# Splitting fp32 weights into hi and lo: by VectorE, or by two transfers and ScalarE

## The chip, the cores and the metric

The kernel runs on 1 core of one Trainium2 chip. The time is device microseconds of one execution; the time before is 799.55 us, the median of 3 runs (799.49 to 800.0). Engines are named as in the profile: PE (TensorE), with PEld for its weight loads, DVE (VectorE), ACT (ScalarE), POOL (GpSimd) and SP (SyncE, which only issues transfers).

## What is computed

One post-norm encoder layer on 512 tokens of width 1024, all in float32. Two token mixers work on the same input: windowed grouped-query attention (A) and a mixture of three dilated attentions (B). Sigmoid gates merge them; then a SwiGLU of width 2816.

```python
proj = h @ w_in[l]
qa, ka, va, qb, kb, vb = jnp.split(proj, SPLITS, axis=-1)
...
o_a = windowed_gqa_sink(qa, ka, va, a_sink[l])
o_b = dilated_mixture(qb, kb, vb)
gates = jax.nn.sigmoid(h @ w_gate[l] + b_gate[l])
g_a, g_b = jnp.split(gates, N_BRANCH, axis=-1)
mixed = g_a * (o_a @ w_br_a[l]) + g_b * (o_b @ w_br_b[l])
h = layer_norm(DN_ALPHA * h + mixed @ w_out[l], ln1_g[l], ln1_b[l])
f = (jax.nn.silu(h @ w_ff_gate[l]) * (h @ w_ff_up[l])) @ w_ff_down[l]
h = layer_norm(DN_ALPHA * h + f, ln2_g[l], ln2_b[l])
```

## The kernel before

**Products.** Each operand of a large product is split into two parts that the PE takes in one pass each: hi, the operand rounded to the type float32r, and lo, what is left of it. A product is three matmuls: hi by hi, hi by lo, lo by hi (`feat_k`, lines 432 to 434; in `tok_major`, 959 to 961). So each weight must be split before it is used.

**Weights.** They lie in HBM as units of 128x1024, and a unit is fetched as two half units of 128x512 (256 KB). `half_unit` makes one: SP loads it to a slot of class `ws`, `split` copies it with rounding to h (ACT or DVE, lines 312 and 314), and DVE subtracts h from it into l (line 336). h and l lie in slots of class `whl`. 152 half units go this way: all projections, the gates, the branch and output projections, the first three and the last two of 22 feed-forward blocks, and the last four rows of down units. The first four half units of the program are cut into pieces instead (`half_unit_by`, 355 to 361). Most feed-forward blocks (`quad`) and most down units (`Chunk`) use a Strassen-like scheme with sums of weights: for those, `load_sum` loads one weight and has POOL issue a second transfer that adds another to it (line 326). These remain.

**Order.** No engine's order is written by hand. Operations are recorded with the engines that may do them, costs, priorities and what they read and write; `Program.run` then plays them through by those costs and gives each engine its instructions in the order in which they would start. At run time each engine keeps that order and waits for semaphores. `pr.limits` says how many slots each class may hold at once (85 in all; `N_WS` for `ws`, `N_WHL` for `whl`, the rest for general use), and two operations of no cost change those limits between stages. A half unit's priority is that of a matmul 130 us earlier (`LOOK`).

**Stages**, by the profile: start and first projections, then attention A and B between further projections and gates up to 361 us, branch and output projections with the first layer norm up to about 451, feed-forward blocks, and the last down units with the second layer norm from about 745 on. At the end of the output projection each block of 128 tokens is normalised and turned (`turn_h1`: four PE transposes of line 1026, then ACT and DVE copies), while the PE goes on with the next block.

Of the kernel before, what the change touches and what calls it, by code (L numbers as in the profile page):

```python
# [9 lines left out]
F32 = mybir.dt.float32  # L10
F32R = mybir.dt.float32r
BF16 = mybir.dt.bfloat16
AF = mybir.ActivationFunctionType
ALU = mybir.AluOpType

P = 128
S = 512
# [4 lines left out]
NR = 4  # L22
# [34 lines left out]

FIRST = ((-1000, -998), (-997.5, -996), (-993.5,), (-992.5,),
         (-999, -997, -995, -994, -993, -992, -991, -990))
N_WS, N_WHL, N_ATT = 6, 12, 16  # L60


QUADS = range(3, 20)
# [30 lines left out]
class Program:  # L94
# [15 lines left out]
    def op(self, alts, fn, reads=(), writes=(), prio=0.0, after=(), abs_prio=None, moves=0.0):  # L110
        o = Op()
        o.alts, o.fn = alts, fn
        o.prio = (self.T + prio if abs_prio is None else abs_prio, len(self.ops))
        o.ready, o.done, o.eng = 0.0, None, None
        deps = set(a for a in after if a is not None)
        for t in reads:
            deps.update(self.writer.get(t, ()))
        for t in writes:
            deps.update(self.writer.get(t, ()))
            deps.update(self.readers.get(t, ()))  # L120
        deps.discard(o)
# [12 lines left out]
        o.succ = []  # L134
        o.left = len(deps)
        for d in deps:
            d.succ.append(o)
        self.ops.append(o)
        return o
# [118 lines left out]
def act(n, psum=False, extra=0):  # L258
    return (0.052 if psum else 0.094) + 0.000833 * n + 0.093 * extra
# [11 lines left out]
def hybrid_layer(ctx: ExitStack, tc: tile.TileContext, wpack, xT, xtok, sink, bgate,  # L271
                 ln1g, ln1b, ln2g, ln2b, ropec, ropes, maska, maskb, identd, out):
    nc = tc.nc
# [9 lines left out]
    op = pr.op  # L283
# [7 lines left out]
    def slot(dt=F32, cls=None):  # L291
        cls = cls or "gen"
        return Buf("slot", cls, lambda: slab.tile([P, S], dt, tag="slab", bufs=N_SLOT, name=name("sl")))
# [16 lines left out]
    def copy(eng, dst, src):  # L310
        if eng == ACT:
            nc.scalar.activation(dst, src, AF.Copy)  # L312
        else:
            nc.vector.tensor_copy(dst, src)

    def f32(ap):
        return ap.bitcast(F32)

    def load(b, src, cost=0.73, prio=0.0, abs_prio=None, dst=None, after=()):
        return op([(SP, cost)], lambda e: nc.sync.dma_start(dst() if dst else b.t, src), writes=[b],  # L320
                  prio=prio, abs_prio=abs_prio, after=after)
# [7 lines left out]
    def cp_alts(n, ps=False):  # L329
        return [(ACT, act(n, ps)), (DVE, dve(n, not ps))]  # L330

    def split(src, h, l, prio=0.0, abs_prio=None, hold=()):

        op(cp_alts(S), lambda e: copy(e, h.t, src.t), reads=[src], writes=[h, *hold], prio=prio,
           abs_prio=abs_prio)
        op([(DVE, dve(S))], lambda e: nc.vector.tensor_tensor(l.t, src.t, f32(h.t), op=ALU.subtract),  # L336
           reads=[src, h], writes=[l], prio=prio, abs_prio=abs_prio)
# [1 line left out]
    LOOK, LOOK_W, LOOK_U, LOOK_T = 130.0, 30.0, 15.0, 15.0  # L339

    def half_unit(u, j):
        st, h, l = slot(F32, "ws"), slot(F32R, "whl"), slot(F32R, "whl")
        load(st, wpack[u, :, j * S:(j + 1) * S], prio=-LOOK)
        split(st, h, l, prio=-LOOK, hold=[(l, "room")])
        return h, l

    pieces = {}

    def half_unit_by(u, j, cuts, prios):

        st, h, l = slot(F32, "ws"), slot(F32R, "whl"), slot(F32R, "whl")
        pieces[h] = pieces[l] = cuts
        for (c0, c1), ap in zip(cuts, prios):
            w = c1 - c0
            op([(SP, 0.73 * w / S)], lambda e, c0=c0, c1=c1: nc.sync.dma_start(
                st.t[:, c0:c1], wpack[u, :, j * S + c0:j * S + c1]), writes=[(st, c0)], abs_prio=ap)
            op(cp_alts(w), lambda e, c0=c0, c1=c1: copy(e, h.t[:, c0:c1], st.t[:, c0:c1]),
               reads=[(st, c0)], writes=[(h, c0), (l, "room", c0)], abs_prio=ap)
            op([(DVE, dve(w))], lambda e, c0=c0, c1=c1: nc.vector.tensor_tensor(
                l.t[:, c0:c1], st.t[:, c0:c1], f32(h.t[:, c0:c1]), op=ALU.subtract),  # L360
               reads=[(st, c0), (h, c0)], writes=[(l, c0)], abs_prio=ap)
        return h, l
# [471 lines left out]
    def dense_k(u, nt):  # L834
        ps = bank("dense")
        feat_x(ps, unit(u))
        return k_post(ps, nt)
# [12 lines left out]
    def step(w):  # L850
        if w == "VA":
            env["va"] = turned_values(U_VA, 4)
        elif w[0] == "q":
            i = int(w[1])
            kv = (i // 2) % 2
            qa.extend(dense_q(U_QA + i, 4, (kv, kv)))
        elif w == "k1":
            ka.extend(dense_k(U_KA + 1, 4))
        elif w[0] == "A":
            g = int(w[1])  # L860
            for b in range(NR):
                unit_a(g, b, qa[4 * g:4 * g + 4], ka[g], env["va"])
        elif w[0] in "gG":
            for _ in range(int(w[1:] or 1)):
                gate(env["gate"], w[0] == "G")
                env["gate"] += 1
        elif w[0] in "QK":
            pair, g = int(w[1]), int(w[2])
            u = U_QKB + 6 * pair + 2 * g + (w[0] == "K")
            if w[0] == "Q":  # L870
                env["qs"][pair, g] = dense_q(u, 4 if g == 0 else 0, (0, 1))
            else:
                env["ks"][pair, g] = dense_k(u, 8 if g == 0 else 0)
        elif w == "V0":
            env["v0"] = turned_values(U_V0, 8, 1)
        elif w[0] == "V":
            env["v" + w[1]] = token_values(U_VB + 2 * int(w[1]) - 2)
        elif w[0] == "B":
            hs = int(w[1])
            unit_b(hs, [env["qs"][hs // 2, g][hs % 2] for g in range(3)],  # L880
                   [env["ks"][hs // 2, g][hs % 2] for g in range(3)], env["v0"], env["v1"], env["v2"])
# [4 lines left out]
    op([(POOL, 0.0)], lambda e: pr.limits.update(gen=N_SLOT - N_WS - N_WHL, whl=max(N_WHL, 4 * N_LAST1 + 4)), after=lasts)  # L886


    def split_of(src, toks, prio=0.0):
        h, l = slot(F32R), slot(F32R)  # L890
        op(cp_alts(S), lambda e: copy(e, h.t, src.t), reads=toks, writes=[h, (l, "room")], prio=prio)
        op([(DVE, dve(S))], lambda e: nc.vector.tensor_tensor(l.t, src.t, f32(h.t), op=ALU.subtract),
           reads=[*toks, h], writes=[l], prio=prio)
        return h, l
# [8 lines left out]
    for f in range(16):  # L903
        op([(ACT, act(S))], lambda e, f=f: nc.scalar.activation(gz[f].t, gz[f].t, AF.Sigmoid),
           reads=[gz[f]], writes=[gz[f]], after=exps)
    sa = [split_of(t, [(t, b) for b in range(NR)], -20) for t in oaT]
    MA = moving(sa)
    sm = []
    mark = None
# [543 lines left out]
```

## Time and profile before

| | |
|---|---|
| median of 3 runs | 799.55 us |
| profiled execution, its time | 799.82 us |
| its span, first to last instruction | 797.7 us |
| PE, DVE, ACT, POOL busy | 98%, 83%, 56%, 11% |
| DMA queue of SP: data, share of 16 engines | 91.53 MB, 35.0% |
| DMA queue of POOL: data, share of 16 engines | 13.63 MB, 10.4% |

Busy times by stretch, and the share of the 16 DMA engines:

| us | DVE | ACT | POOL | DMA |
|---|---|---|---|---|
| 0 to 437 | 351.92 | 264.86 | 46.20 | 0.35 |
| 437 to 490 | 48.96 | 29.90 | 6.13 | 0.57 |
| 490 to 740 | 221.23 | 145.93 | 37.21 | 0.71 |
| 740 to 798 | 41.14 | 9.22 | 0.00 | 0.10 |

How to read it: matmuls are pipelined, and one counts as busy while its columns run through, so 98% doesn't say that the PE issues all the time; what its weight loads waited for says more. The granted clock was full almost throughout (0.996). The share of the DMA engines is a mean over the stretch.

### The profile page before, as it was taken

The page shows a single profiled execution, that of the slowest core. Times are in us where ns is not written, and L with a number is a line of the kernel's source. Part 1 is how long each engine was busy: PE and PEld are TensorE (multiplying, and loading weights), DVE is VectorE, ACT ScalarE, POOL GpSimd, SP SyncE. Part 2 cuts the span into 40 slices and gives each one's busy share as a digit, 9 for nine tenths or more (in the row PEclk, how much of TensorE's full clock was granted, in tenths as well). Part 3 has the DMA queues.
Part 4 walks back from the last instruction along what each step waited for, and adds up shares of the span by engine and source line. Part 5 has one row for each costly group of instructions (what it writes and reads, how often), then busy time and mean ns, then how long its engine had stood idle before and what let it go on. Part 6 is the DMA issues. An engine that isn't in the chain of part 4 may idle for free.

```text
span 797.7 us, 13253 instructions
## 1 busy us (share of the span) xinstructions
PE 784.7 (98%) x4598; PEld 690.3 (87%) x4598; DVE 663.3 (83%) x1385; ACT 449.9 (56%) x980; POOL 89.5 (11%) x256
## 2 busy tenths in 40 slices
PE   8999999999999999999999999999999999999995
PEld 5888888888899888888888899999999999998884
DVE  6998989999955699858495988699898989898858
ACT  5577665758755663767151555555556546566310
POOL 0000000000033100420000011111121211100000
PEclk9999999999999999999999999999999999999998
DMA  8423132242032132328442458666986857846002
GB/s 291 171 93 102 55 109 67 80 146 66 27 106 68 51 107 68 122 91 306 155 144 68 135 143 199 158 171 151 227 224 173 204 147 209 242 153 178 1 19 87
DMA packets 58674, 106.00 MB, mean 133 GB/s; under 512 B 6768, under 2 KB 7792, under 8 KB 58608
## 3 DMA queue, kind: packets, MB, share of 16 engines
q1 hardware_dynamic: 51120, 91.53, 35.0%
q0 software_dynamic: 7488, 13.63, 10.4%
q8 instruction: 36, 0.59, 0.3%
q14 instruction: 30, 0.25, 0.1%
HBM read 100.68 MB, written 4.46 MB: 132 GB/s over the span
## 4 chain that ended last, share of the span: by engine, by line
PE 89%; DVE 6%; ACT 2%; DMA 1%; issue 1%; SPq 0%; DVEq 0%; ACTq 0%
PE ps L433 13%; PE ps L432 13%; PE ps L434 13%; PE ps L1156 7%; PE ps L1155 7%; PE ps L1154 7%; PE ps L1293 4%; PE ps L1294 4%; PE ps L1295 4%; PE ps L608 3%; PE ps L961 2%; PE ps L959 2%; PE ps L960 2%; PE ps L517 2%; PE ps L516 2%; ACT sl L312 1%
## 5 line engine op out<-in xcount | busy, mean ns | idle before, releaser
L312 ACT ACTIVATE sl<-sl 128x512 fp32r<-128x512 f32 (+3 forms) x404 | 226.4, 593 | 102.2 <-DVE sl L458 42.9
L432 PE MATMUL ps<-x,sl 128*128 128x512 f32 (+1 forms) x464 | 174.4, 376 | 0.6 <-ACT x L312 0.6
L433 PE MATMUL ps<-x,sl 128*128 128x512 f32 (+1 forms) x464 | 171.5, 370 | 0.2 <-DVE x L408 0.2
L434 PE MATMUL ps<-x,sl 128*128 128x512 f32 (+1 forms) x464 | 171.1, 369 | 0.0
L312 ACT ACTIVATE sl<-ps 128x256 f32<-128x256 f32 (+5 forms) x169 | 76.3, 468 | 116.4 <-PE ps L1156 72.6
L1065 DVE TENSOR_TENSOR sl<-sl,sl 128x512 fp32r<-128x512 f32 (+3 forms) x246 | 137.9, 599 | 4.6 <-ACT sl L312 3.3
L336 DVE TENSOR_TENSOR sl<-sl,sl 128x512 fp32r<-128x512 f32 x152 | 101.4, 686 | 6.0 <-ACT sl L312 3.7
L434 PEld LDWEIGHTS ps<-x,sl 128*128 128x128 f32 x464 | 87.6, 189 | 15.0
L432 PEld LDWEIGHTS ps<-x,sl 128*128 128x128 f32 x464 | 87.8, 189 | 13.5 <-ACT x L312 1.7
L433 PEld LDWEIGHTS ps<-x,sl 128*128 128x128 f32 x464 | 87.8, 189 | 13.1 <-DVE x L408 1.4
L1156 PE MATMUL ps<-sl,sl 128*128 128x256 f32 x272 | 77.0, 283 | 0.0
L1155 PE MATMUL ps<-sl,sl 128*128 128x256 f32 x272 | 77.0, 283 | 0.0
L1154 PE MATMUL ps<-sl,sl 128*128 128x256 f32 x272 | 77.0, 283 | 0.0
L326 POOL DMA_DIRECT2D sl<-wpack x34 | 29.5, 867 | 281.9 <-PE ps L960 75.2
L1156 PE MATMUL ps<-x,sl 128*128 128x256 f32 x204 | 57.7, 283 | 0.0
L1155 PE MATMUL ps<-x,sl 128*128 128x256 f32 x204 | 57.7, 283 | 0.0
L1154 PE MATMUL ps<-x,sl 128*128 128x256 f32 x204 | 57.7, 283 | 0.0
L1154 PEld LDWEIGHTS ps<-sl,sl 128*128 128x128 f32 x272 | 52.2, 192 | 0.2
L1155 PEld LDWEIGHTS ps<-sl,sl 128*128 128x128 f32 x272 | 52.2, 192 | 0.2
L1156 PEld LDWEIGHTS ps<-sl,sl 128*128 128x128 f32 x272 | 52.2, 192 | 0.0
L1293 PE MATMUL ps<-sl,sl 128*128 128x512 f32 x126 | 49.3, 391 | 0.0
L1294 PE MATMUL ps<-sl,sl 128*128 128x512 f32 x126 | 49.3, 391 | 0.0
(135 smaller groups left out, 1623.4 us busy)
## 6 DMA issues: line engine op xcount, KB each, us to landing
sl<-wpack SPq DMA_DIRECT2D x239, 256.0 KB, 3.5
wf<-wpack SPq DMA_DIRECT2D x54, 256.0 KB, 4.3
sl<-wpack POOLq DMA_DIRECT2D x34, 256.0 KB, 5.2
wf<-wpack POOLq DMA_DIRECT2D x18, 256.0 KB, 7.0
gz<-sl SPq DMA_DIRECT2D x9, 256.0 KB, 2.1
sl<-gz SPq DMA_DIRECT2D x9, 256.0 KB, 4.7
sl<-xT SPq DMA_DIRECT2D x8, 256.0 KB, 5.5
sl<-xtok SPq DMA_DIRECT2D x8, 256.0 KB, 5.3
```

The costliest lines, as they stand in the source:

```text
L312: nc.scalar.activation(dst, src, AF.Copy)
L336: op([(DVE, dve(S))], lambda e: nc.vector.tensor_tensor(l.t, src.t, f32(h.t), op=ALU.subtract), reads=[src, h], writes=[l], prio=prio, abs ...
L432: mm(o, a, x0, start=(k == 0), stop=False)
L433: mm(o, a, x1, start=False, stop=False)
L434: mm(o, b, x0, start=False, stop=(k == nk - 1))
L1065: op([(DVE, dve(w))], lambda e: nc.vector.tensor_tensor(dst(), x(), y(), op=o), reads=reads, writes=writes, prio=prio)
L1154: mm(o, wh, bh[k](), start=(first and k == 0), stop=False, skip_group_check=True)
L1155: mm(o, wh, bl[k](), start=False, stop=False, skip_group_check=True)
L1156: mm(o, wl, bh[k](), start=False, stop=(k == 3), skip_group_check=True)
L1293: mm(ps.t, x0, w[0].t, start=(first and m == 0), stop=False, skip_group_check=True)
L1294: mm(ps.t, x0, w[1].t, start=False, stop=False, skip_group_check=True)
L1295: mm(ps.t, x1, w[0].t, start=False, stop=(m == N_PAIR - 1), skip_group_check=True)
```

## The change

A half unit no longer uses a `ws` slot, SP, or DVE. POOL issues a transfer that casts the weight from float32 to float32r on its way into h. ACT writes -h into l (`activation` with scale -1). POOL then issues a second transfer of the same weight that adds it to l, so l is w - h. Each of the three waits for the one before. `N_WS` goes from 6 to 0 and `N_WHL` from 12 to 16; pieces of the first half units take general slots. The splits of A's outputs now also wait for the K projection of the second pair of B heads.

```diff
-N_WS, N_WHL, N_ATT = 6, 12, 16
+N_WS, N_WHL, N_ATT = 0, 16, 16
...
     def half_unit(u, j):
-        st, h, l = slot(F32, "ws"), slot(F32R, "whl"), slot(F32R, "whl")
-        load(st, wpack[u, :, j * S:(j + 1) * S], prio=-LOOK)
-        split(st, h, l, prio=-LOOK, hold=[(l, "room")])
+
+        h, l = slot(F32R, "whl"), slot(F32R, "whl")
+        src = wpack[u, :, j * S:(j + 1) * S]
+        op([(POOL, 1.0)], lambda e: nc.gpsimd.dma_start(h.t, src), writes=[h, (l, "room")], prio=-LOOK, moves=0.73)
+        op([(ACT, act(S))], lambda e: nc.scalar.activation(l.t, f32(h.t), AF.Copy, scale=-1.0), reads=[h],
+           writes=[l], prio=-LOOK)
+        op([(POOL, 1.0)], lambda e: nc.gpsimd.dma_start(l.t, src, accum_op=ALU.add), reads=[l], writes=[l],
+           prio=-LOOK, moves=0.73)
         return h, l
...
     def half_unit_by(u, j, cuts, prios):
-        st, h, l = slot(F32, "ws"), slot(F32R, "whl"), slot(F32R, "whl")
+        st, h, l = slot(F32, "xs"), slot(F32R, "whl"), slot(F32R, "whl")
...
                 env["ks"][pair, g] = dense_k(u, 8 if g == 0 else 0)
+                env["k", pair, g] = pr.ops[-1]
...
-    sa = [split_of(t, [(t, b) for b in range(NR)], -20) for t in oaT]
+    sa = [split_of(t, [(t, b) for b in range(NR)], -20, [env["k", 1,0]]) for t in oaT]
```

In the changed kernel the cast is line 345, the negation 346, the adding transfer 348; lines further down stand 5 or 6 later than before. How instructions stand on two engines at two places:

ACT at the start, before. `sl` slots fed from `wpack` are weights, `x` is the input; each row waits for a load of SP (DMAHW).

```order
L312 ACTIVATE sl20_121<-sl1_72 128x128 [waits DMAHW0_49]
L312 ACTIVATE x422_127<-sl2_74 128x512 [waits DMAHW1_49]
L312 ACTIVATE sl20_121<-sl1_72 128x384 [waits DMAHW2_49]
L312 ACTIVATE sl24_132<-sl3_77 128x128 [waits DMAHW3_49]
L312 ACTIVATE x422_127<-sl4_79 128x512 [waits DMAHW4_49]
L312 ACTIVATE sl24_132<-sl3_77 128x384 [waits DMAHW5_49]
```

The same in the changed kernel; DMASW is a transfer issued by POOL.

```order
L312 ACTIVATE sl26_129<-sl3_75 128x128 [waits DMAHW0_49]
L312 ACTIVATE x428_135<-sl4_77 128x512 [waits DMAHW1_49]
L346 ACTIVATE sl2_73<-sl1_72 128x512 [waits DMASW0_49]
L312 ACTIVATE sl32_144<-sl5_80 128x128 [waits DMAHW3_49]
L312 ACTIVATE x428_135<-sl6_82 128x512 [waits DMAHW4_49]
L312 ACTIVATE sl32_144<-sl5_80 128x384 [waits DMAHW5_49]
```

A negation of a weight that is used later stands third, ahead of the first piece of the q weights and the second tile of x.

ACT before, at the end of the output projection: `ps1114` is a turned half of the second token block, `ps1140` of the third; the rows from `sl1115` on copy feed-forward weights to h.

```order
L312 ACTIVATE sl1111_4966<-ps1114_5010 128x2x128
L312 ACTIVATE sl1115_5039<-sl1086_4808 128x512
L312 ACTIVATE sl1117_5046<-sl1087_4817 128x512
L991 ACTIVATE st1113_5008<-st1113_5008,eps_68 128x1
L312 ACTIVATE sl1119_5055<-sl1092_4836 128x512
L312 ACTIVATE sl1121_5062<-sl1093_4841 128x512
L312 ACTIVATE sl1124_5071<-sl1098_4872 128x512
L312 ACTIVATE sl1127_5080<-sl1099_4877 128x512
L312 ACTIVATE sl1132_5101<-sl1123_5065 128x512
L312 ACTIVATE sl1136_5112<-sl1126_5074 128x512
L312 ACTIVATE sl1138_5122<-sl1129_5083 128x512
L312 ACTIVATE sl1142_5136<-sl1130_5089 128x512
```

The same place in the changed kernel: `ps982` is a half of the second block, `ps991` and `ps995` are those of the third.

```order
L312 ACTIVATE sl979_4828<-ps982_4872 128x2x128
L997 ACTIVATE st981_4870<-st981_4870,eps_68 128x1
L312 ACTIVATE x4970_4801<-ps991_4932 128x4x128
L346 ACTIVATE sl984_4902<-sl983_4901 128x512
L312 ACTIVATE sl996_4957<-ps991_4932 128x2x128
L346 ACTIVATE sl986_4911<-sl985_4910 128x512
L312 ACTIVATE sl997_4965<-ps991_4932 128x2x128
L312 ACTIVATE sl998_4967<-ps995_4947 128x2x128
L346 ACTIVATE sl988_4922<-sl987_4921 128x512
L312 ACTIVATE sl1000_4979<-ps995_4947 128x2x128
L346 ACTIVATE sl990_4930<-sl989_4929 128x512
L346 ACTIVATE sl994_4945<-sl993_4944 128x512
```

Before, ten weights were copied ahead of the third block's turn; now five negations stand among its copies. Only two half units of this stage are negated earlier.

More of the change, by code (lines that the diff above doesn't have):

```diff
@@ L886, in hybrid_layer, with split_of @@
     op([(POOL, 0.0)], lambda e: pr.limits.update(gen=N_SLOT - N_WS - N_WHL, whl=max(N_WHL, 4 * N_LAST1 + 4)), after=lasts)
-    def split_of(src, toks, prio=0.0):
+    def split_of(src, toks, prio=0.0, after=()):
         h, l = slot(F32R), slot(F32R)
-        op(cp_alts(S), lambda e: copy(e, h.t, src.t), reads=toks, writes=[h, (l, "room")], prio=prio)
+        op(cp_alts(S), lambda e: copy(e, h.t, src.t), reads=toks, writes=[h, (l, "room")], prio=prio, after=after)
         op([(DVE, dve(S))], lambda e: nc.vector.tensor_tensor(l.t, src.t, f32(h.t), op=ALU.subtract),
```

## The prediction

> **What bounds the kernel now.** The page first: how long the span is, who fills it, and on what the chain that ended last lies.
>
> ```profile
> span 797.7 us, 13253 instructions
> ...
> PE 784.7 (98%) x4598; PEld 690.3 (87%) x4598; DVE 663.3 (83%) x1385; ACT 449.9 (56%) x980; POOL 89.5 (11%) x256
> ...
> PE 89%; DVE 6%; ACT 2%; DMA 1%; issue 1%; SPq 0%; DVEq 0%; ACTq 0%
> ```
>
> TensorE holds the chain, but VectorE (DVE) is 83% busy and has 6% of it, so relief of VectorE could be worth something. How much, the waits of TensorE's weight loads (PEld) say: a matmul that has to wait shows there first. Columns: who waited, for whom, us in total, times, longest.
>
> ```profile
> PEld ps L608 <- ACT sl L596: 2.3, 6, 1.0
> PEld ps L432 <- ACT x L312: 1.7, 2, 1.0
> ...
> PEld ps L433 <- DVE x L408: 1.4, 3, 0.5
> ...
> PEld ps L654 <- DVE sl L613: 1.1, 3, 0.4
> PEld ps L1026 <- DVE sl L1008: 0.8, 2, 0.4
> PEld ps L777 <- DVE sl L613: 0.7, 1, 0.7
> PEld ps L802 <- DVE sl L613: 0.5, 1, 0.5
> ```
>
> L432 and L433 wait at the start, for x; L1026 waits in the first layer norm, which the change leaves alone. What is left hangs on the attention's elementwise chain: 2.3 + 1.1 + 0.7 + 0.5 = 4.6 us. That is the whole room below: the chain's 6% on VectorE runs beside matmuls that go on issuing. Stretches of 20 us show the same (TensorE, its weight loads, DVE, ACT, POOL busy, then clock, DMA share and GB/s):
>
> ```profile
> 180.00:200.00 20.00, 19.90 (x93) 16.03 (x92) 19.59 (x41) 16.83 (x32) 1.59 (x4) 1.00 0.20 66
> 200.00:220.00 20.00, 19.26 (x109) 16.44 (x108) 18.52 (x45) 14.55 (x35) 0.61 (x4) 1.00 0.10 27
> ...
> 400.00:420.00 20.00, 20.00 (x90) 16.54 (x89) 16.87 (x28) 9.49 (x16) 0.00 (x0) 1.00 0.48 159
> 420.00:440.00 20.00, 20.00 (x93) 16.27 (x91) 12.08 (x21) 2.97 (x8) 1.87 (x2) 1.00 0.24 52
> ```
>
> VectorE is full at 180 to 220, and TensorE still issues; at 400 to 440 nothing holds it. So a late weight costs its full lateness, and nothing later gives it back.
>
> **What is removed.** For each of 152 half units (128x512 weights) a load on SP's queue, one copy and one VectorE subtraction:
>
> ```profile
> L336 DVE TENSOR_TENSOR sl<-sl,sl 128x512 fp32r<-128x512 f32 x152 | 101.4, 686 | 6.0 <-ACT sl L312 3.7
> ...
> sl<-wpack SPq DMA_DIRECT2D x239, 256.0 KB, 3.5
> ```
>
> 101.4 us leave VectorE. The copies become negations on ScalarE (ACT), one for one, so its load stays. Of the 4.6 us above, 2.3 have ScalarE as releaser, and it stays as loaded; the other 2.3 wait for VectorE's L613. I take -3.0 for the relief, with 0 and -4.6 as ends: what is late next there is ScalarE's softmax.
>
> **What is added.** 304 transfers on POOL's queue, two in series for each half unit with a ScalarE instruction between. The nearest rows are the present accumulating transfers (L326): POOL's time for an issue, then issue to landing (min/median/max), and what the two queues' packets took.
>
> ```profile
> L326 POOL DMA_DIRECT2D sl<-wpack x34: 862/862/1007, 421.1 to 677.1; - x34
> L326 POOL DMA_DIRECT2D wf<-wpack x18: 862/865/1294, 476.0 to 720.3; - x18
> ...
> DMA to landing us min/median/max: 3.7/5.5/9.7
> ...
> q1 hardware_dynamic: 51120, 91.53, 35.0%
> q0 software_dynamic: 7488, 13.63, 10.4%
> ...
> L312 ACT ACTIVATE sl<-sl 128x512 fp32r<-128x512 f32 x282 | 166.7, 623 | 50.8 <-DVE sl L929 16.7 <-DVE sl L1191 8.1 <-DVE sl L1065 7.3
> ```
>
> A weight is then ready 5.5 + 0.62 + 5.5 = 11.6 us after its first issue, against 3.5 + 0.62 + 0.69 = 4.8 now. POOL: 304 x 0.86 = 261 us over the span, so it isn't full. The transfers: 35.0% of 797.7 us for 91.53 MB is 3.05 us/MB, 0.80 us of all 16 engines for a plain 256 KB; 10.4% for 13.63 MB is 1.60 us for an accumulating one. No row shows a casting transfer: 0.80 is its lower end, 1.60 its upper. It moves the bytes of a plain one and reads no destination, so I take 0.80. A half unit then needs 2.40 us of the engines, and TensorE uses one up in 12 matmuls of 512 columns. Their pace is in the chain's pieces (start, us, what):
>
> ```profile
> 444.16 0.23 PE ps L959
> ...
> 219.51 0.12 PE ps L581
> ...
> 441.65 0.44 PE ps L1026 x4
> ```
>
> 12 x 0.23 = 2.76 us, more where attention lies between. It fits, at 87% of the engines in the dense stretches. There the lead decides. By the changed order an accumulating transfer is mostly released 20 to 30 us of TensorE's work ahead of its use, against some 8 us (negation, issue, landing): these cost nothing while the lead holds. Four places have less.
>
> *Start.* ScalarE's second copy is now followed by a negation that waits for the first casting transfer, ahead of the q weights' first piece and the second x tile. What gates TensorE there now:
>
> ```profile
> 0.75 0.38 SPq L355 DMA_DIRECT2D sl<-wpack  x1
> ...
> 5.47 0.31 ACT L312 ACTIVATE sl<-sl 128x128 fp32r<-128x128 f32 x1 [0.36 <-DMA sl<-wpack]
> ...
> 7.12 0.63 ACT L312 ACTIVATE x<-sl 128x512 fp32r<-128x512 f32 x1 [1.34 <-DMA sl<-xT]
> ...
> 4.00:6.00 2.00, 2.00 (x5) 0.87 (x4) 1.34 (x3) 1.38 (x3) 0.00 (x0) 1.00 0.84 243
> 6.00:8.00 2.00, 1.43 (x6) 0.84 (x4) 0.33 (x2) 0.88 (x2) 0.00 (x0) 1.00 0.92 281
> ```
>
> Issued at about 1 us, as SP's first is at 0.75, and landed 5.5 later, with 0.62 and 0.31 of ScalarE: x can be copied at 7.4 instead of 7.1, if it is there. With 9.7 it is 11.6, 4.5 late. The engines are 84 to 92% busy then, and five casting transfers (1.3 MB) join the x loads. I take +2.0, between 0 and +4.5.
>
> *Branch projections.* The last attention head is done some 15 us of TensorE's work ahead of the first use of the add released by it; POOL's queue then has nine casting transfers ahead of the next adds, beside the 21 loads of gates, x and layer norm vectors. 5 x 1.60 + 9 x 0.80 is 15 us of engine time, and half of the 21 loads 8: 23 us against 26 to the use of the tenth. Each add still lands late after that: +1.0, 0 to +4.
>
> *Into the feed-forward part.* This is the largest. Before, ScalarE had copied these weights ahead of the third token block's turn; now five negations stand behind that block's copies. From the block's transposes to the first matmul that reads the first of these lo parts, TensorE's order has 12 matmuls of 512, one more group of four transposes and 26 matmuls of 256: 12 x 0.23 + 0.44 + 26 x 0.12 = 6.3 us. Against that the turn's copy 0.60 (quoted next), a negation 0.62, and the landing.
>
> ```profile
> L312 ACT ACTIVATE x<-ps 128x512 fp32r<-128x512 f32 x8 | 4.8, 598 | 13.2 <-PE ps L1026 13.2
> ```
>
> With 5.5 that is 6.7, 0.4 us late; with 9.7 it is 10.9, 4.6 late. SP's queue holds 19 loads for the feed-forward part right behind the layer norm vectors, with nothing but free buffers to hold them, so I go near the contended end: +4.0. Five more follow at 12 x 0.12 = 1.44 us each in the first pass, about as fast as an add moves (1.60): the upper end is +8.
> [...]
>
> *Last down weights.* Four adds are released 7.9 to 10 us ahead; a subtraction, a split copy, a negation and a landing make 0.69 + 0.62 + 0.62 + 5.5 = 7.4. The engines are idle there: +0.3, 0 to +2.
>
> SP loses 152 loads, which only brings its later loads forward. The 18 + 34 accumulating loads of the feed-forward part keep more than 30 us of lead. POOL's small attention copies now stand between transfers and wait for softmax; their waits are inside the leads above. That some gates' splits now also wait for a K projection costs nothing: that is long done.
>
> **Sum**, against the profiled execution's own 799.82 (797.7 of span and 2.1 around it): 799.82 - 3.0 + 2.0 + 1.0 + 4.0 + 0.3 = 804.1. It was 0.27 above the median of 799.55, so 803.9, said as 804.
>
> **Rivals.**
> *The leads hold (faster, 0.24).* Landings stay near 5.5 everywhere, the start loses 0.3, the feed-forward entry 0.4, and the relief brings up to 4.6: 799.6 - 4.6 + 0.7 = 795.7. For it: the median landing; VectorE full at 180 to 220. It decides at a landing of about 6 us: below, the relief is larger than the lateness.
> *They cancel (0.14).* Terms of 2 to 4 us both ways: 798.0 to 801.1, within 0.2% (1.6 us), about what a measurement of this kernel can tell from no change.
> *A casting transfer moves like an accumulating one (slower, 0.07).* Then a half unit needs 3.20 us against 2.76. From the branch projections to the feed-forward part 28 casting and 27 adding transfers and 21 loads make 55 x 1.60 + 21 x 0.80 = 105 us in about 87 of TensorE's work: 18 us more, 822. Against it: it reads no destination.
> *VectorE's copies hold up POOL's issues (slower, 0.03).* An issue took at most 1.29 us against 0.86, so the trace bears out 0.4. Were it several times that at each of the three tight places, with five adds in a row, it would be 10 us: 814.
> [...]
> That the change doesn't do what it says is no rival: the order shows 152 subtractions fewer on VectorE.
>
> **How the numbers follow.** The forecast itself has 0.52, and its band is 801.2 to 814. Faster is the first rival, 0.24. Same is 0.14. Slower is 0.52 + 0.07 + 0.03 = 0.62. The range runs from 796.5 to 814: it takes in the slower ends of the start, branch and feed-forward terms singly, not all together (818), and leaves out 822 and the best of the first rival.
>
> **What would show it.** VectorE's busy time near 562 us with L336's group gone; POOL's issues 356; TensorE waiting for DMA landings at 5 to 12 us, around 365 to 380 and at 445 to 455; its waits at 188 to 212 and 360 shrunk. It is wrong if no weight load waits for a landing of wpack, if the waits in the attention grow (ScalarE queued behind late casting transfers), or if landings on POOL's queue have a median above 8 us through the whole first half.

## The result, and the profile after

The changed kernel takes 847.54 us (median of 4 runs, 842.3 to 849.08) against 799.75 beside it: a ratio of 1.0588, 95% interval 1.0572 to 1.0604, so 48 us slower where 4 were forecast. The profiled execution took 849.08 us. Its page: span, busy time by engine, the two data queues (packets, MB, share of 16 engines), and the shares of the chain that ended last.

```profile
span 847.2 us, 13441 instructions
...
PE 808.2 (95%) x4598; PEld 706.2 (83%) x4598; DVE 580.0 (68%) x1237; ACT 451.0 (53%) x976; POOL 297.8 (35%) x560
...
q0 software_dynamic: 51264, 93.35, 55.7%
q1 hardware_dynamic: 29232, 51.67, 18.5%
...
PE 54%; issue 15%; DMA 10%; POOL 9%; DVE 7%; ACT 4%; SPq 1%; POOLq 0%; DVEq 0%; ACTq 0%
```

The change did to VectorE what it says: 663.3 us became 580.0 (83 less, not the 101 of the subtractions: its copies, L314, took some 7 us more, and the rest was not followed up). But TensorE's share of the chain fell from 89% to 54%, and landings and GpSimd, which had 1% and nothing, have 19%. The waits of the changed kernel (who, for whom, us in total, times, longest):

```profile
POOL sl L348 <- ACT sl L346: 220.8, 76, 19.4
ACT sl L346 <- DMA sl<-wpack: 101.3, 45, 6.9
...
DVE st L747 <- POOL st L740: 28.5, 4, 16.4
...
PEld ps L439 <- DMA sl<-wpack: 7.6, 3, 3.4
...
PEld ps L613 <- ACT sl L601: 6.5, 9, 2.7
...
PEld ps L966 <- DMA sl<-wpack: 6.0, 4, 3.6
...
PEld ps L521 <- issue: 4.7, 1, 4.7
```

Read from the top it looks like a chain of queues: the add (L348) holds GpSimd for the negation, the negation (L346) holds ScalarE for the cast's landing, VectorE's merge of attention B (L747) waits for GpSimd's small copies (L740), and TensorE waits for all three: for landed weights (L439, L966), for softmax (L613) and for A's first scores (L521). Not every wait in it costs time: the longest of VectorE's four for L740, 16.4 us, ended at 288 us, in a stretch that lost nothing. In stretches of the changed kernel (TensorE, its loads, DVE, ACT, POOL, clock, DMA share, GB/s):

```profile
0.00:20.00 20.00, 14.92 (x39) 8.02 (x40) 7.99 (x17) 8.19 (x14) 5.01 (x12) 1.00 0.99 302
40.00:60.00 20.00, 15.66 (x67) 13.04 (x66) 10.17 (x29) 10.38 (x27) 10.56 (x21) 0.83 0.81 171
320.00:340.00 20.00, 17.70 (x92) 15.03 (x90) 13.45 (x36) 14.06 (x31) 8.46 (x16) 0.85 0.86 156
380.00:400.00 20.00, 16.58 (x74) 14.07 (x73) 12.12 (x27) 15.45 (x30) 4.55 (x8) 0.74 0.82 227
440.00:460.00 20.00, 16.95 (x75) 13.70 (x73) 1.41 (x3) 5.24 (x9) 9.82 (x13) 1.00 0.88 183
480.00:520.00 40.00, 32.96 (x219) 30.85 (x218) 24.12 (x40) 17.52 (x35) 18.46 (x23) 0.91 0.99 255
```

The first and the last of these stretches in the kernel before:

```profile
0.00:20.00 20.00, 18.00 (x64) 11.94 (x65) 12.32 (x24) 11.70 (x19) 1.22 (x12) 1.00 0.87 291
...
480.00:520.00 40.00, 40.00 (x336) 40.00 (x335) 30.43 (x57) 22.92 (x49) 6.04 (x7) 1.00 0.77 181
```

TensorE issued 39 matmuls instead of 64 in the first 20 us, and 219 instead of 336 at 480 to 520. The clock, 1.00 before, was granted at 0.74 to 0.91 in four of these stretches.

A finer measure is used below for every kernel: the distance between the starts of neighbouring matmuls, less a base (0.2265 us at 512 columns, 0.116 at 256, 0.0625 at 128), summed where it is over 0.02 us. The medians of the kernel before are 0.227, 0.120 and 0.109, so the base at 128 is an allowance of the author's that stands well below the measured pace. What lies at 1.6 to 2.2 times the base, in matmuls of 256 and 512 columns, counts as slow pace (in brackets), the rest as waits. Matmuls of 128 columns at half pace (0.21 us apart at 334 to 335 us in the changed kernel, 0.11 at 346 to 347) are among the waits, so the brackets are a lower bound. Much of 60 to 310 is the normal pace of short matmuls and transposes: of the 16.1 us of the kernel before, some 9.5 are distances at 128 columns that lie less than 0.1 us above the base. Stretches are fixed in time, so in a shorter kernel an event can slide over an edge.

| kernel | median us | 0–60 | 60–310 | 310–400 | 400–530 | 530 on | of it slow pace |
|---|---|---|---|---|---|---|---|
| before | 799.6 | 6.2 | 16.1 | 6.1 | 2.3 | 0 | (3.3) |
| changed | 847.5 | 18.8 | 14.4 | 25.6 | 18.3 | 2.3 | (13.9) |
| e1 real landing times | 833.5 | 15.0 | 15.1 | 15.8 | 12.0 | 1.1 | (10.1) |
| e2 merge copies on VectorE | 843.6 | 18.7 | 21.5 | 11.4 | 22.8 | 0.8 | (15.2) |
| e3 first units old way | 845.1 | 14.4 | 16.0 | 25.9 | 16.6 | 0.9 | (12.4) |
| e5 = e1 + e2 | 833.9 | 15.7 | 19.3 | 9.5 | 14.6 | 1.2 | (9.3) |
| e6 cast alone | 810.4 | 15.6 | 15.9 | 7.8 | 2.8 | 0 | (5.8) |
| e7 add alone | 810.0 | 10.7 | 16.0 | 5.5 | 5.4 | 1.3 | (4.0) |
| e8 = e3 + x first | 833.2 | 5.7 | 15.4 | 28.0 | 17.6 | 0.8 | (11.1) |
| e9 late units old way | 835.1 | 19.0 | 20.2 | 23.4 | 2.4 | 0 | (10.2) |
| e10 all four cures | 805.4 | 6.0 | 19.4 | 9.6 | 2.4 | 0 | (3.2) |
| e11 middle only | 799.2 | 5.5 | 15.8 | 5.8 | 2.3 | 0 | (3.4) |
| e12 cast alone, x first | 799.5 | 5.8 | 16.1 | 6.4 | 2.7 | 0 | (3.5) |
| e13 landing 10 us | 843.3 | 19.9 | 18.2 | 14.3 | 15.7 | 1.8 | (12.1) |
| e14 = e10, copies on GpSimd | 809.6 | 5.4 | 15.5 | 17.5 | 2.4 | 0 | (4.5) |

The changed kernel's row is 48.7 us above that of before, its span 49.5. So the loss lies in three places: the first 60 us (+12.6), 310 to 400 (+19.5), and 400 on (+18.3). In the middle it gained 1.7. Of the whole, at least 10.6 us are slow pace. The granted clock gives another figure: its mean was 0.971 over 847.2 us and 0.996 over 797.7 us before, so 24.6 and 3.2 us of full clock were withheld. By that up to some 21 us of the loss can be slow pace; this is an estimate, and the half pace of the first microseconds (matmuls of 512 columns 0.43 us apart at 11.4 to 12.7 us, where the granted clock reads 1.00) is not in it.

### The profile page after: what moved, and what is told of

Same layout as the page of the kernel before. It is cut to its first block, busy times and chain, and to the rows that moved or that the text cites. A ratio compares the mean times of both kernels' runs of the same rounds, so it can differ in the third digit from the quotient of the medians.

```text
span 847.2 us, 13441 instructions
## 1 busy us (share of the span) xinstructions
PE 808.2 (95%) x4598; PEld 706.2 (83%) x4598; DVE 580.0 (68%) x1237; ACT 451.0 (53%) x976; POOL 297.8 (35%) x560
## 4 chain that ended last, share of the span: by engine, by line
PE 54%; issue 15%; DMA 10%; POOL 9%; DVE 7%; ACT 4%; SPq 1%; POOLq 0%; DVEq 0%; ACTq 0%
DMA sl<-wpack 9%; PE ps L1162 7%; PE ps L1161 7%; PE ps L1160 7%; PE ps L437 6%; PE ps L439 6%; PE ps L438 6%; POOL sl L348 4%; POOL sl L345 3%; PE ps L1300 3%; PE ps L1299 3%; PE ps L1301 3%; ACT sl L312 2%; PE ps L613 2%; DMA sl<-xT 1%
## 5 line engine op out<-in xcount | busy, mean ns | idle before, releaser
L348 POOL DMA_DIRECT2D sl<-wpack x152 | 136.5, 973 | 292.9 <-ACT sl L346 220.8
L312 ACT ACTIVATE sl<-sl 128x512 fp32r<-128x512 f32 (+3 forms) x261 | 142.7, 576 | 78.0 <-DVE sl L463 28.0
L439 PE MATMUL ps<-x,sl 128*128 128x512 f32 (+1 forms) x464 | 174.8, 377 | 7.0 <-DMA sl<-wpack 7.0
L437 PE MATMUL ps<-x,sl 128*128 128x512 f32 (+1 forms) x464 | 178.0, 384 | 2.2 <-DVE sl L314 1.9
L438 PE MATMUL ps<-x,sl 128*128 128x512 f32 (+1 forms) x464 | 175.2, 378 | 1.7 <-DVE x L413 1.7
L346 ACT ACTIVATE sl<-sl 128x512 fp32r<-128x512 f32 x152 | 93.8, 625 | 102.3 <-DMA sl<-wpack 101.3
L345 POOL DMA_DIRECT2D sl<-wpack x152 | 116.1, 940 | 13.6 <-DMA sl<-wpack 5.6
L312 ACT ACTIVATE sl<-ps 128x256 f32<-128x256 f32 (+6 forms) x157 | 69.9, 457 | 94.9 <-PE ps L1162 69.7
L439 PEld LDWEIGHTS ps<-x,sl 128*128 128x128 f32 x464 | 90.4, 195 | 23.4 <-DMA sl<-wpack 7.6
L437 PEld LDWEIGHTS ps<-x,sl 128*128 128x128 f32 x464 | 90.2, 194 | 16.9 <-issue 2.3
L438 PEld LDWEIGHTS ps<-x,sl 128*128 128x128 f32 x464 | 90.3, 195 | 15.2 <-DVE x L413 3.1
L326 POOL DMA_DIRECT2D sl<-wpack x34 | 29.7, 963 | 164.2 <-DMA sl<-wpack 62.0
```

Source lines behind the costliest of these rows:

```text
L326: op([(POOL, 1.0)], lambda e: nc.gpsimd.dma_start(b.t, src2, accum_op=ALU.add), reads=[b], writes=[b], prio=prio, moves=1.65)
L345: op([(POOL, 1.0)], lambda e: nc.gpsimd.dma_start(h.t, src), writes=[h, (l, "room")], prio=-LOOK, moves=0.73)
L346: op([(ACT, act(S))], lambda e: nc.scalar.activation(l.t, f32(h.t), AF.Copy, scale=-1.0), reads=[h], writes=[l], prio=-LOOK)
L348: op([(POOL, 1.0)], lambda e: nc.gpsimd.dma_start(l.t, src, accum_op=ALU.add), reads=[l], writes=[l], prio=-LOOK, moves=0.73)
L437: mm(o, a, x0, start=(k == 0), stop=False)
L438: mm(o, a, x1, start=False, stop=False)
```

## How the three places lose

**ScalarE at 40 to 53 us.** ScalarE's rows, then VectorE's, then TensorE's, of the changed kernel (start, us, what, idle before and its releaser):

```profile
40.84 1.95 ACT L346 ACTIVATE sl<-sl 128x512 fp32r<-128x512 f32 x3 [6.28 <-DMA sl<-wpack]
...
49.00 0.63 ACT L346 ACTIVATE sl<-sl 128x512 fp32r<-128x512 f32 x1 [5.39 <-DMA sl<-wpack]
50.99 0.63 ACT L346 ACTIVATE sl<-sl 128x512 fp32r<-128x512 f32 x1 [1.37 <-DMA sl<-wpack]
51.53 0.61 ACT L312 ACTIVATE sl<-sl 64x512 fp32r<-64x512 f32 x1
...
52.17 0.69 DVE L487 TENSOR_TENSOR sl<-sl,sl 64x512 fp32r<-64x512 f32 x1 [3.71 <-ACT sl L312]
...
48.28 0.39 PE L439 MATMUL ps<-x,sl 128*128 128x512 f32 x1
53.01 0.55 PE L521 MATMUL ps<-sl,sl 128*128 128x256 f32 x1 [4.34 <-DVE sl L487]
...
53.58 0.63 PE L437 MATMUL ps<-x,sl 128*128 128x512 f32 x1
54.00 0.63 PE L438 MATMUL ps<-x,sl 128*128 128x512 f32 x1
```

A copy of a rotated Q (51.53) needs no weight, yet it stands behind two negations whose casts have not landed; VectorE needs the copy, TensorE needs VectorE. The weights negated are for later. And the matmuls behind the wait are 0.42 apart, not 0.23.

**GpSimd at 376 to 385.** GpSimd, VectorE, TensorE:

```profile
376.70 0.86 POOL L348 DMA_DIRECT2D sl<-wpack  x1 [2.00 <-ACT sl L346]
377.24 0.89 POOL L345 DMA_DIRECT2D sl<-wpack  x1
378.18 0.18 POOL L739 COPY st<-st 32x2 f32<-32x2 f32 x1
...
379.64 0.18 POOL L740 COPY st<-st 32x2 f32<-32x2 f32 x1
...
379.85 0.17 DVE L747 TENSOR_TENSOR st<-st 128x8 f32<-128x8 f32 x1 [6.62 <-POOL st L740]
...
385.30 2.61 PE L613 MATMUL ps<-ident,sl 128*128 128x128 f32 x11 [2.38 <-ACT sl L601]
```

The last eight of the 32 small copies wait behind an add that waits for a negation; the merge, the scaling of the probabilities (L601) and TensorE's transposes follow.

**ScalarE again at 326, and half pace behind both.** ScalarE, then TensorE; then two stretches in the columns used above:

```profile
325.82 0.63 ACT L346 ACTIVATE sl<-sl 128x512 fp32r<-128x512 f32 x1 [2.99 <-DMA sl<-wpack]
...
332.27 0.33 PE L781 MATMUL ps<-sl,sl 128*128 128x128 f32 x1 [1.61 <-ACT sl L312]
...
334.00:344.00 10.00, 10.00 (x42) 9.42 (x42) 2.53 (x13) 6.31 (x20) 5.17 (x21) 0.50 0.60 113
385.00:395.00 10.00, 8.66 (x33) 7.50 (x33) 6.97 (x12) 9.06 (x19) 3.17 (x5) 0.51 0.75 184
```

Here TensorE waits for ScalarE's copy of turned probabilities, not for a merge: ScalarE had lost 3 us to a cast and then worked without a gap until 333 us. Of the 25.6 us of this stretch of the table, 11.9 lie at 320 to 350 and 13.8 at 360 to 400. In the two windows the clock was half, and 18.7 us of TensorE's work would have taken half of that at the full clock (an estimate): about 9 of the 19.5 us lost at 310 to 400 are slow pace, most of it in matmuls of 128 columns.

**Output projection.** ScalarE, GpSimd and TensorE there:

```profile
452.05 0.63 ACT L346 ACTIVATE sl<-sl 128x512 fp32r<-128x512 f32 x1 [6.87 <-DMA sl<-wpack]
...
452.99 0.89 POOL L348 DMA_DIRECT2D sl<-wpack  x1 [4.22 <-ACT sl L346]
...
456.56 0.39 PE L965 MATMUL ps<-sl,sl 128*128 128x512 f32 x1
460.14 0.74 PE L966 MATMUL ps<-sl,sl 128*128 128x512 f32 x1 [3.19 <-DMA sl<-wpack]
```

Here the weights themselves are late: TensorE's next matmul (L966, the one that reads lo) starts 3.35 us late, for an add that lands.

## Experiments

The theory: negations and adds stand in the order where the planner (`Program.run`) reckons a landing about 3.9 us after the issue (1.0 for the issue, 0.73 moved, 2.0, and 0.2 for the step to another engine), while the trace has a median of 5.9 for casts and 4.7 for adds, at most 15.3 and 12.8; queues that run in order then hold everything behind. The rival: the transfers themselves, by their number, time or share of the engines.

**e1, real landing times in the planner.**

```diff
-                        o.done = dma[1] + 2.0
+                        o.done = dma[1] + (4.2 if o.moves < 1.0 else 2.0)
```

> The changed kernel, with one number of the planner altered: it reckons a half unit's transfer as landed 4.2 us after it moved instead of 2.0, so about 6 us after the issue, as the trace of the changed kernel shows (median 5.9 for the cast, 4.7 for the add), instead of 3.9. Theory 1 (the loss is made by in-order queues: a negation stands on ScalarE where its cast has not landed, an add on GpSimd where its negation is not done, and all behind them wait): the wait of 4.5 us at 48 us goes, and so does most of the loss at 30 to 60 and 440 to 530: 815 to 830 us. Theory 2 (the transfers themselves are too slow or too many, wherever they are put): within 5 us of 847.

833.52 us (ratio 1.0421, 1.0405 to 1.0436): 14 us back, just short of the range. The wait at 48 us is gone, and ScalarE's waits for casts fell from 101.3 to 57.8 us.

**e2, merge copies on VectorE.**

```diff
-                    nc.gpsimd.tensor_copy(st.t[x, 12 + r:29 + r:16], st.t[y, b:17 + b:16])
-                    nc.gpsimd.tensor_copy(st.t[y, 8 + b:25 + b:16], st.t[x, 4 + r:21 + r:16])
+                    nc.vector.tensor_copy(st.t[x, 12 + r:29 + r:16], st.t[y, b:17 + b:16])
+                    nc.vector.tensor_copy(st.t[y, 8 + b:25 + b:16], st.t[x, 4 + r:21 + r:16])
-            op([(POOL, 2.07)], cross, reads=[(st, w, i) for w in "ml" for i in range(8)],
+            op([(DVE, 0.7)], cross, reads=[(st, w, i) for w in "ml" for i in range(8)],
```

> The changed kernel, with the 128 small copies of attention B's merge on VectorE instead of GpSimd. Theory 1 (on GpSimd they stand behind transfers that wait, so the softmax merge comes late and TensorE waits at 310 to 400): the loss there, about 17 us with the slow pace behind it, goes: 828 to 834, and no wait of VectorE for L740. Rival (the merge is late because ScalarE is held by late casts, GpSimd's copies only follow): 842 to 848.

843.59 us. Two stretches of it:

```profile
320.00:340.00 20.00, 20.00 (x90) 16.57 (x89) 15.90 (x29) 8.93 (x15) 9.50 (x14) 1.00 0.86 171
380.00:400.00 20.00, 20.00 (x92) 16.62 (x91) 4.84 (x8) 6.92 (x13) 10.00 (x16) 1.00 1.08 279
```

At both places TensorE no longer waits, and 310 to 400 lost 14.2 us less, as the theory says. Yet the total fell by 4: the copies cost 7 us more at 60 to 310 (where two of the four heads merge), and 400 to 530 lost 4.5 us more. The time lies in the rival's range. Two things weaken the test: on VectorE eight copies took 1.3 us where the edit reckons 0.7, and at 285 us TensorE waits 2.15 us for VectorE behind them; and the whole order moved, so that the wait at 332 went too doesn't show that the copies had made it. At 380 the place is supported, the size is not.

**e3, first units the old way**: the first four Q, V of A and two gates use SP, copy and subtraction, with 3 slots for loads (`N_WS` 3).

```diff
     def half_unit(u, j):
+        if u in OLD:
+            st, h, l = slot(F32, "ws"), slot(F32R, "whl"), slot(F32R, "whl")
+            load(st, wpack[u, :, j * S:(j + 1) * S], prio=-LOOK)
+            split(st, h, l, prio=-LOOK, hold=[(l, "room")])
+            return h, l
```

> The changed kernel, with the units used in about the first 50 us (first four Q, both V, two gates) split the old way: load by SP, copy, subtraction by VectorE, with 3 slots for loads. Theory (start and the wait at 48 us are made by these weights and lie on top of the rest): the loss at 0 to 60, about 15 us with the slow pace, falls to 3: 833 to 837. Rival (the loss moves to the first units behind them): 843 to 848.

845.06 us: the rival. The long wait at 48 us went, but not that of the first 20 us, where casts for later units now ran beside x.

**e4, what a wait costs beyond its length.** In the kernel before, ahead of the first product of groups 2, 4 and 6 of the branch projections:

```diff
+            def hold(e, z=z, ps=last_ps, l=wu[0][1], n=HOLD[f]):
+                nc.scalar.activation(z.t[:, 0:1], ps.t[:, 0:1], AF.Copy)
+                for _ in range(n):
+                    nc.scalar.activation(l.t, f32(l.t), AF.Copy)
+            op([(ACT, 0.0)], hold, reads=[last_ps], writes=[z, wu[0][1]], prio=-1000)
```

> The kernel before, with three waits made on purpose in the branch projections: ahead of the groups 2, 4 and 6 ScalarE copies one lo weight onto itself 1, 3 and 8 times, so TensorE waits about 0.8, 2.1 and 5.2 us there. It measures what one wait of TensorE costs beyond its own length. If a wait costs its length: about +8 us, and matmuls of 512 columns go on at 0.23 us. If the clock is lowered after a long wait, as the changed kernel's rows at 53 us suggest (0.43 us a matmul): no such matmuls behind the first wait, about 4 us of them (some 2 us lost) behind the third, the second is open: +10 to +12.

807.25 us, 7.7 above before. Only the wait of 8 copies reached TensorE; the two shorter ones did not show (none over 0.46 us). TensorE around the long one:

```profile
385.10 0.39 PE L435 MATMUL ps<-sl,sl 128*128 128x512 f32 x1
389.77 0.80 PE L436 MATMUL ps<-sl,sl 128*128 128x512 f32 x1 [4.28 <-ACT sl L921]
390.36 0.63 PE L434 MATMUL ps<-sl,sl 128*128 128x512 f32 x1
390.79 0.63 PE L435 MATMUL ps<-sl,sl 128*128 128x512 f32 x1
...
392.49 0.61 PE L436 MATMUL ps<-sl,sl 128*128 128x512 f32 x1
392.92 0.41 PE L434 MATMUL ps<-sl,sl 128*128 128x512 f32 x1
393.17 0.40 PE L435 MATMUL ps<-sl,sl 128*128 128x512 f32 x1
```

Distance 4.67 instead of 0.23, then 0.59, then six of 0.43: a wait of 4.4 us costs 6.0; the rest of the 7.7 was not placed. For 3.1 us after it the matmuls run at half pace. In the changed kernel at 334 to 344 the clock stayed at 0.50 for some 10 us while 42 matmuls, most of 128 columns, kept TensorE busy, after gaps of 1.9 and 0.8 us.

**e5, e1 and e2 together.**

> The changed kernel with both: the planner reckons a half unit's transfers 2.2 us longer (the first run, 833.5), and attention B's merge copies are on VectorE (the second run, 843.6). If the two cure different waits they add up: 847.5 - 14.0 - 4.0 = 829.5. If the wait of 10 us at 345 to 380 that the first run still had belongs to the copies on GpSimd: 821 to 826. If the order by real landing times had already freed the copies: 833.

833.85 us: they do not add up. It is the time of the third case, but not for its reason: 310 to 400 did fall from 15.8 to 9.5, so the copies had not been free; it was given back at 60 to 310 (+4.2) and behind (+2.6).

**e6, the cast alone** (slots as before):

```diff
-        h, l = slot(F32R, "whl"), slot(F32R, "whl")
+        st, h, l = slot(F32, "ws"), slot(F32R, "whl"), slot(F32R, "whl")
         src = wpack[u, :, j * S:(j + 1) * S]
         op([(POOL, 1.0)], lambda e: nc.gpsimd.dma_start(h.t, src), writes=[h, (l, "room")], prio=-LOOK, moves=0.73)
-        op([(ACT, act(S))], lambda e: nc.scalar.activation(l.t, f32(h.t), AF.Copy, scale=-1.0), reads=[h],
-           writes=[l], prio=-LOOK)
-        op([(POOL, 1.0)], lambda e: nc.gpsimd.dma_start(l.t, src, accum_op=ALU.add), reads=[l], writes=[l],
-           prio=-LOOK, moves=0.73)
+        load(st, src, prio=-LOOK)
+        op([(DVE, dve(S))], lambda e: nc.vector.tensor_tensor(l.t, st.t, f32(h.t), op=ALU.subtract),
+           reads=[st, h], writes=[l], prio=-LOOK)
```

> One part of the change alone: h by GpSimd's casting transfer, but w loaded by SP as before and l made by VectorE's subtraction; ScalarE does nothing for weights, 152 transfers on GpSimd, none of which waits for ScalarE; slots as before (6 for loads, 12 for h and l). Theory 1 (the series of two landings with ScalarE between, and the queues it holds up, makes the loss): 805 to 818, TensorE's waits at the start stay, those at 310 to 400 go. Rival (casting transfers in themselves, by their time or by the engines they share with SP's loads): 830 or more.

**e7, the add alone** (slots as before):

```diff
-        h, l = slot(F32R, "whl"), slot(F32R, "whl")
+        st, h, l = slot(F32, "ws"), slot(F32R, "whl"), slot(F32R, "whl")
         src = wpack[u, :, j * S:(j + 1) * S]
-        op([(POOL, 1.0)], lambda e: nc.gpsimd.dma_start(h.t, src), writes=[h, (l, "room")], prio=-LOOK, moves=0.73)
+        load(st, src, prio=-LOOK)
+        op(cp_alts(S), lambda e: copy(e, h.t, st.t), reads=[st], writes=[h, (l, "room")], prio=-LOOK)
         op([(ACT, act(S))], lambda e: nc.scalar.activation(l.t, f32(h.t), AF.Copy, scale=-1.0), reads=[h],
            writes=[l], prio=-LOOK)
```

> The other part alone: w loaded by SP and rounded to h by a copy as before, then ScalarE writes -h to l and GpSimd's transfer adds w; no casting transfers, 152 more ScalarE instructions than in the changed kernel; slots as before. ScalarE's negation then waits for a copy, not for a cast's landing. Theory 1: what held ScalarE is gone, adds on GpSimd wait for little: 803 to 815, late adds at the output projection remain (landing). Rival (the adds' landings make most of the loss): 825 or more.

810.39 and 809.98 us (ratios 1.0136, 1.0119 to 1.0153, and 1.0125, 1.011 to 1.014). Each half costs 10 to 11 us, both 48: what is lost beyond 21 comes only with both. That it comes from the series is the likely reading, not a shown one: both together also put twice as many transfers on GpSimd's queue (304 against 152), and the slots differ. e7 has as many adds as the changed kernel and 54 us more work on ScalarE (505.2 against 451.0), and at 310 to 400 it waits less than the kernel before. e6 lost nearly all of its 11 us in the first 30 us. Its queue on GpSimd also prices the cast:

```profile
q0 software_dynamic: 29376, 53.49, 27.8%
```

27.8% of its span of 808.8 is 224.9 us; the 52 adds among it take 13.63 MB x 6.09 us/MB (10.4% of 797.7 for 13.63 MB, before) = 83.0, so 152 casts take 141.9: 0.93 us of the engines for 256 KB (an estimate: it takes the adds at their price before), against 0.80 for a plain transfer and 1.60 for an add.

**e8, x first**: e3, and GpSimd copies one element of the last x tile ahead of its first cast.

```diff
-        op([(POOL, 1.0)], lambda e: nc.gpsimd.dma_start(h.t, src), writes=[h, (l, "room")], prio=-LOOK, moves=0.73)
+        op([(POOL, 1.0)], lambda e: nc.gpsimd.dma_start(h.t, src), writes=[h, (l, "room")], prio=-LOOK, moves=0.73, after=[held])
...
+    held = op([(POOL, 0.1)], lambda e: nc.gpsimd.tensor_copy(xin.t, f32(xl[KD - 1]()[:, 0:1])),
+              reads=xtok_of(KD - 1), writes=[xin], abs_prio=-990)
```

> The third run's kernel (first units split the old way, 845.1), with GpSimd's first casting transfer held until the last x tile is there (a copy of one element from it stands first on GpSimd). Theory (the start is lost because casting transfers share the DMA engines with the x loads, whose landing grew from 5.5 to 8.9 us): x lands near 5.5 again, the start's 8.4 of waits and 3.6 of slow pace fall to the 2.5 and 1.8 of before: 837 to 840. Rival (the negation ahead on ScalarE, or lateness handed on to later units): 843 to 847.

833.16 us (ratio 1.0427, 1.0392 to 1.0462), 12 below e3 and better than expected. The traces show less: 8.7 us less in the first 60 us, 2.1 and 1.0 more at 310 to 400 and 400 to 530. e8's runs lie between 831.0 and 837.1 us, and the profiled one is the slowest, so its gain beyond the start is not placed. The x loads' landing (min/median/max) in the changed kernel, then in e8:

```profile
DMA to landing us min/median/max: 2.6/8.9/10.2
```

```profile
DMA to landing us min/median/max: 2.6/5.2/5.9
```

The hold also moves the first negation on ScalarE behind x. But e6 has no negations, and there x landed as late (median 9.9 us) and the start lost 10.5 us. So the start is lost to casts that run beside the x loads.

**e9, late units the old way**: `OLD` holds output projection, feed-forward and down; slots are given out in the order of use.

> The changed kernel, with all half units of the output projection, the feed-forward and the down blocks split the old way (SP, copy, VectorE), 3 slots for loads; slots for h and l are given out in the order of use. Theory (the loss at 440 to 530, 17 us with the slow pace, and the 2 at the end belong to the adds of these units, too close to their use): 827 to 832. Rival (the loss is handed on from the branch part): 838 or more.

835.09 us. The stretch that issued 219 matmuls now issues 313, at full clock:

```profile
480.00:520.00 40.00, 40.00 (x313) 38.70 (x312) 35.80 (x65) 21.69 (x45) 6.03 (x7) 1.00 0.72 191
```

400 to 530 fell from 18.3 to 2.4 and the end lost nothing; the total fell by 12.5, not 18, with more lost at 60 to 310 (part of it a wait of 2.1 us at 306.6 for ScalarE's copy of turned probabilities, behind a cast: what the changed kernel has at 332).

**e10, all four cures**: e1, e2, e8 and e9 in one. Here and in e11 and e12 slots are given out as in e9.

> All cures at once: first units by the old way and GpSimd's transfers held until x is there, the late units by the old way, the planner with real landing times, attention B's merge copies on VectorE. The new way is left for the units used from about 60 to 440 us, 65 of the 152 or more. If the four places are the whole loss: start -7, 30 to 60 -5, 310 to 400 -17, 440 on -19: 799 to 803. If series and queues lose wherever they run: 808 or more.

805.43 us (ratio 1.0074, 1.006 to 1.0088): 42 of 48 us are back, 2.4 short of the range.

**e11, the middle only**: the new way for 48 half units used at about 60 to 290 us; e1's landing times; x first; `N_WS` 4 and `N_WHL` 14.

> The new way only for the units used from about 60 to 290 us (gates 2 to 8, the second K of A, four Q of A, the first pair of B and its values), the planner with real landing times, GpSimd held until x is there; everything else as before, merge copies on GpSimd. In the changed kernel this stretch alone lost nothing (waits and slow pace 14.4 us at 60 to 310, 16.1 in the kernel before). Theory: 1 to 2 us faster than before, 797.5 to 799. Rival (GpSimd's merge copies at 260 to 290 and the hand-over cost as much): 800 to 804.

799.23 us (ratio 0.9995, 0.9986 to 1.0004): no difference. With enough lead the new way costs nothing, but VectorE's 20 us less (643.1) bring nothing either.

**e12, cast alone with x first**: e6, the first units the old way, casts and their loads held for x.

> The cast-alone kernel (810.4), with the first units split the old way, and casts and their loads held until x is there. It lost 10.5 us in the first 30 us and nothing much later. Theory (that loss is x landing late, 9.9 us, beside the casts): 799 to 802. Rival (a cast is late by itself for the first units that use it): 805 or more.

799.49 us (ratio 1.0002, 0.9993 to 1.0011). The cast's 11 us were the start alone; that first units and hold were changed together leaves open how much each gave. This kernel has 13 us less work on VectorE and 53 less on ScalarE (650.2 and 396.9), for the same time.

**e13, landing of 10 us in the planner**: e1 with 8.4 in place of 4.2.

> The first run's kernel with a longer landing: the planner reckons 8.4 us behind the move, so about 10 us from the issue, above nearly all landings (median 5.9 and 4.7, longest 15). If the size of the planner's error sets how long negations and adds hold ScalarE and GpSimd: 847.5 at 3.9 us, 833.5 at 6, and now 818 to 828, with ScalarE's wait for casts (101 us in the changed kernel, 58 in the first run) below 25. If 6 us was enough and what is left is the start (sharing of the DMA engines) and adds too close to their use: 830 to 837.

843.29 us: neither. ScalarE's waits for casts fell again, to 36.9 us, and the time rose. A new wait of 5.3 us stands at 25 us, where this order puts A's first scores (35.6 us in the kernel before). So the first theory holds as to which waits exist, but the time does not follow the planner's error: a later negation also spends the add's lead, and one cost changed moves the whole order.

**e14, e10 with the merge copies on GpSimd.**

> The kernel of the four places (805.4) with attention B's merge copies back on GpSimd. It had waits of 18.4 us at 60 to 310 where the changed kernel had 14.0, as the two other runs with these copies on VectorE had (19.4, 18.6). If the copies on VectorE make that: 60 to 310 back to 14 to 15, 800 to 803, unless GpSimd's queue brings back waits at 310 to 400: then 805 to 810.

809.58 us. 60 to 310 fell from 19.4 to 15.5, so the copies on VectorE make 3.9 of the 5.9 us that e10 still lost. But 310 to 400 rose from 9.6 to 17.5: GpSimd's queue brought back one wait, behind copies that stand between adds (VectorE's merge had waited 3.25 us for them):

```profile
355.31 0.39 PE L453 MATMUL ps<-sl,sl 128*128 128x512 f32 x1
360.98 0.45 PE L627 MATMUL ps<-ident,sl 128*128 128x128 f32 x1 [5.28 <-DVE sl L617]
```

No version beat the kernel before: e11 and e12 equal it.

## Why the prediction failed, step by step

**"Now stand between transfers and wait for softmax; their waits are inside the leads" is the step that failed.** It looked at the transfers that wait for the copies, and not at the copies that wait for the transfers. The softmax of the last two heads has no lead: merges held by GpSimd for 4.85 us (at 356) and 6.62 us (at 380) were followed by waits of TensorE (0.66 us at 362, 2.38 us at 385). 310 to 400 lost 19.5 us where the sum had nothing. About half of it, at 360 to 400, stands behind these merges; e14 against e10 shows what copies in GpSimd's queue cost there (7.9 us).

**ScalarE held by late casts** was named as what would make the forecast wrong, and had a term at two places only. At 48 us it cost some 5 us. The other half of the loss at 310 to 400, at 320 to 350, stands behind such a wait too (the row at 326); no run changes that wait alone.

**Leads of 20 to 30 us.** They were read from the order as if each queue ran freely. Adds wait for negations (220.8 us on GpSimd), negations for casts; the lead is spent before the add is issued.

**Start: +2.0, at most +4.5; measured +7.4** (0 to 30 us). The term took one casting transfer in ScalarE's way; what counts is x's landing, which rose from 5.5 to 8.9 us (e6 and e8). The engines' 84 to 92% share, which it quoted, was the sign.

**Into the feed-forward part: +4.0, at most +8; measured +16 from 400 to 530.** The place was right (e9), and the step it describes came nearly as sized: the negations stand behind the third block's copies, and TensorE waited 3.2 us for the first lo part, whose add GpSimd had issued at 485.9, about 8 us earlier.

```profile
494.04 0.39 PE L439 MATMUL ps<-x,sl 128*128 128x256 f32 x1 [3.24 <-DMA sl<-wpack]
```

Another wait of 3.05 us, at 510.8 for the adds behind, is within its upper end. What the term lacked is a wait of 3.35 us in the output projection itself (the rows at 452) and the slow pace after each (clock 0.57 at 460 to 464 and at 494 to 498, 0.61 at 510.7 to 514).

**Branch projections +1.0: nothing** was lost at 400 to 440. **Last down weights +0.3: 2.** **Relief -3.0:** 1.7 at 60 to 310 in the changed kernel, and in e11 nothing that can be measured. In these runs the room of 4.6 us was not to be had by lighter VectorE alone.

**"A late weight costs its full lateness": more than that.** e4 has 6.0 us for a wait of 4.4. Slow pace is 10.6 to some 21 of the 49 us, and the sum had no term for it. The prediction's own evidence was that nothing later gives a wait back; it did not ask what a wait adds.

**Rivals.** A cast moves for 0.93 us (e6, estimated), so not like an add; the sum's 0.80 was near. Why an add takes twice a plain transfer (1.60 against 0.80) no run shows. GpSimd's issue has a median of 0.88 us against 0.86; single ones took up to 2.59 (L326); whether VectorE's copies made them long, and what they cost, was not tried. "The leads hold" is refuted: landings took up to 15.3 us, and what waited for the landings held the queues.

What stays open: how the loss divides between queues that are held and leads that are too short where both occur. e1 and e13 move both at once. Open too is how much of the loss beyond 21 us belongs to the series and how much to twice the transfers.

## What to carry to other kernels

Before work moves to a queue, list what already stands in that queue and who waits for it: an instruction with no lead (a softmax step) behind one that waits for a landing can become a wait of the critical engine (here 2.38 us of TensorE at 385). Price two parts of a change together as well as apart; together they lost 48 us where each alone lost 10. And an order planned with a landing of 3.9 us did not hold where the medians were 4.7 and 5.9 us and the longest 15.3; reckoning 10 us for all was no cure either (e13).

## What the runs showed of the hardware

A wait of TensorE of 4.4 us was followed by 3.1 us of matmuls at half pace (e4: 512 columns, 0.43 us apart instead of 0.23). Behind waits of 0.8 us at 211 us in the kernel before and of 0.9 us at 211 in the changed one, the next two matmuls of 512 columns start 0.31 us apart and those behind them 0.23. Behind gaps of 1.9 and 0.8 us at 330 to 333 in the changed kernel the clock was 0.50 for some 10 us (334 to 344), with TensorE at work. A plain transfer of 256 KB takes 0.80 us of the 16 engines and an adding one 1.60 (before), a casting one 0.93 (e6, estimated with the adds at their price before). Casts issued beside the x loads moved x's median landing from 5.5 us (before) to 8.9 (changed; 9.9 in e6); it was 5.2 with the casts held for x (e8).
